# A reserve at each hand-over, and longer GpSimd steps, in a kernel whose instruction order is computed

## Chip, core and metric

The kernel runs on one NeuronCore of a Trainium2 chip. The engines named below are TensorE (PE in the profile; its weight loads are a row of their own, PEld), VectorE (DVE), ScalarE (ACT), GpSimd (POOL), and SyncE (SP), which issues most of the transfers. The metric is the device time of one execution in microseconds (us); lower is better.

## What is computed

The reference is one encoder layer on 256 tokens of width 2048, in f32, cut here to its steps:

```python
h = rms_norm(x, g_mix);  c_q, c_kv, k_rope, dq, dk, dv = split(h @ w_in)
q  = rms_norm(c_q) @ w_uq;  kv = rms_norm(c_kv) @ w_ukv        # the latents
out_mla  = softmax attention, 8 heads, rope on part of q and on k_rope
o_diff   = (softmax(q1 k1) - lam * softmax(q2 k2)) @ dv;  out_diff = rms_norm(o_diff)   # 4 heads
x = x + concat(out_mla, out_diff) @ w_out
x = x + cross_attention(rms_norm(x), rms_norm(mem)) @ w_xo     # 4 heads, 256 memory tokens
hf = rms_norm(x);  x = x + (silu(hf @ w_gate) * (hf @ w_up)) @ w_down        # hidden width 5632
return rms_norm(x)
```

## The kernel before

**Three matmuls for one product.** Every f32 operand is split in two: a high part, which is the operand rounded to the narrower type fp32r, and a low part, the remainder. A product is high x high + low x high + high x low, each a matmul with 128 rows of weights and up to 512 columns. For a weight tile the load lands in `wraw` (three buffers), ScalarE writes the high part `wh` (a CAST), VectorE subtracts to get the low part `wl` (a TENSOR_TENSOR). `wh` and `wl` have four buffers each. So each piece of weights goes DMA, ScalarE, VectorE, TensorE. The activations are split likewise: `cqT_h` and `cqT_l`, `forms_h` and `forms_l`, and so on.

**Plain and wide pieces.** A piece of kind P is used as it is. In a piece of kind W, four 512-column blocks of weights are combined into sums, `tsum` on VectorE, so that seven block products stand for eight; four of those products gather in their own PSUM tiles `q1`, `q5`, `q7`, `q6`, which VectorE later adds into the result (`left`, or `res` in the gate and up products). The sums have a longer way: DMA, VectorE (`tsum`), ScalarE (`wh<-tsum`), VectorE (`wl<-tsum`), TensorE. The last two sums of a piece use a pair of buffers of their own, `wh2` and `wl2`, shown by the profile as `wh` and `wl`. The activations that belong to W pieces have sums too (`sums`, `forms`).

**Stages.** From the start to some 40 us the input projection onto the latents; to 65 us the first differential query (`x0T` times `w_in`), beside which the latents are normalised; then MLA heads, differential heads, the output projection (from about 245 us), cross-attention (330 to 460 us), and from 460 us the feed-forward part in six chunks of hidden columns, one narrow and five wide: gate, up, then the down projection after chunks 1, 3 and 5.

**Steps named later.** `rms_rows` scales a latent by `rstd` (`cq<-acc,rstd`, `ckv<-acckv,rstd`), sums its squares on ScalarE (`ss`), adds epsilon on VectorE (`rq<-ss`, `rkv<-ss`), raises to the power -1/2 on GpSimd (`rq<-rq,mhalf`, `rkv<-rkv,mhalf`), and multiplies on VectorE (`cq<-cq,rq`). `transposed` has TensorE turn a tile into a PSUM tile `pt`, out of which VectorE multiplies by a gain (`gT<-pt,gains`) and the split follows. `kr` is the key part with rope; it needs sine and cosine, for which GpSimd computes angles in a long chain (`turns`, `prod`, `ang`) and ScalarE evaluates `sinr` and `cosr`. PSUM tiles for such use come from one ring of four (`pps`), another ring of four (`pacc`) holds the accumulators. In the differential heads `pod` is a head's output, `ssd` its mean square, `rd` the GpSimd power of it, `on` the normalised output, `pdt` its transpose. In a wide chunk, `res` (after silu and product) is turned by TensorE, copied back by ScalarE and split into `hT_h` and `hT_l`.

**What sets the order.** `Plan` records all operations with their needs, and then lays each engine's queue out by list scheduling. `cost` gives an operation the time that it keeps its engine and its lag. The first `run` takes the program's order as priority; it sets the order of matmuls (the `chain`) and which tile takes which buffer. Two more runs follow. For each, `wanted` is worked out from the end backwards: an operation is wanted when the earliest of its users is wanted, less its own lag and a fixed time where the user waits for it. Among the operations that can start within `CHOICE` = 0.3 us of the earliest, the one with the smallest `wanted` goes first. The matmuls keep the order of the run before; TensorE's transposes in the feed-forward part are `free` and find their own place. `HANDOVER` = 0.06 us is also what the simulated queues add when a result passes to another engine. The order that comes out is fixed in the program: on the chip every engine takes its instructions strictly in that order.

Of the kernel before, what the change touches and what calls it, by code (L numbers as in the profile page):

```python
# [178 lines left out]
class Plan:  # L179


    HANDOVER, CHOICE = 0.06, 0.3
    BEGUN = {"tensor": 0.6, "vector": 0.8, "scalar": 0.7, "sync": 0.7, "gpsimd": 0.3}

    def __init__(self, tc):
# [59 lines left out]
    def cost(self, engine, method, out, ins, kw):  # L245
        if method == "dma_start":
            size = max(x.cols() for x in out + ins) * 512
            return {"gpsimd": 0.55, "sync": 0.45, "scalar": 0.45}[engine], 2.0 + size / 375e3, size / 381e3
        n = max([x.cols() for x in out[:1]] + ([x.cols() for x in ins[:1]] if "reduce" in method else []))
        in_psum = bool(ins) and ins[0].tile.whole  # L250
        if engine == "tensor":
            t = 0.108 if method == "transpose" else 0.0134 + n / 2400
            return t, t + 0.14, 0.0
        if engine == "gpsimd":
            if method in ("memset", "affine_select", "tensor_copy"):
                t = 0.1 + n * 1.2e-3
            else:
                t = 0.59 if n == 1 else 0.7 if n == 2 else 1.0
            return t, t + 0.03, 0.0
        if engine == "vector":  # L260
            if n <= 16 and "reduce" not in method:
                t = 0.08
            elif method == "scalar_tensor_tensor":
                t = 0.127 + n * 1.05e-3
            elif method == "tensor_scalar":
                t = 0.129 + n * 1.035e-3 if in_psum else n / 960
            elif method == "tensor_tensor_reduce":
                t = 0.145 + n / 960
            elif method == "tensor_copy":
                t = n / 960  # L270
            else:
                t = 0.068 + n / 960
            return t, t + 0.082, 0.0
        t = 0.044 + 0.855e-3 * n if in_psum else 0.092 + 0.842e-3 * n
        if isinstance(kw.get("scale"), Ref) or isinstance(kw.get("bias"), Ref):
            t += 0.09 if n < 512 else 0.15
        if kw.get("accum_out") is not None:
            t += 0.093
        return t, t + (0.15 if kw.get("accum_out") is not None else 0.08), 0.0

    @contextmanager
    def issue_after(self, op):
        first = len(self.ops)
        yield
        for o in self.ops[first:]:
            if o.engine == op.engine:
                o.after(op, False)

    def run(self, chain, wanted, emit):
        asked = wanted is None  # L290
        for o in self.order:
# [101 lines left out]
    def emit(self, rounds=2):  # L393
        self.order = self.ops
        self.link()
        starts, ended, order = self.run(None, None, False)
        opens = {}
        for o in order:
            for h in o.tiles:
                if h.old is None:  # L400
                    continue
                if h not in opens:
                    opens[h] = done = Op("none", 0.0, 0.0, None)
                    done.number = o.number
                    for x in h.old.ops:
                        done.after(x, True)
                o.after(opens[h], True)
        self.order, seen = [], set()
        for o in order:
            for h in o.tiles:  # L410
                if h in opens and h not in seen:
                    seen.add(h)
                    self.order.append(opens[h])
            self.order.append(o)
        self.link()
        self.log = [ended]
        for n in range(rounds):
            chain = sorted((o for o in self.order if o.engine == "tensor" and not o.free), key=lambda o: starts[o])
            wanted = {}
            for o in reversed(self.order):  # L420
                wanted[o] = starts[o] if o.engine == "tensor" and not o.free else ended
                for x, waits in o.then:
                    wanted[o] = min(wanted[o], wanted[x] - (o.lag + self.HANDOVER if waits else 0.0))
            starts, ended, self.order = self.run(chain, wanted, n == rounds - 1)
            self.log.append(ended)
            self.final = starts
        for p in reversed(self.pools):
            if not p.closed:
                p.shut()
# [1038 lines left out]
```

## Time and profile before

| | |
|---|---|
| time, median of 3 runs | 1146.52 us (1145.23 to 1147.33) |
| the profiled execution | 1146.09 us, span 1144.3 us |
| TensorE matmul busy | 1128.8 us, 99% of the span |
| VectorE busy | 1016.5 us, 89% |
| ScalarE busy | 695.1 us, 61% |
| GpSimd busy | 57.7 us, 5% |
| granted TensorE clock | 0.998 of full speed |

All columns of times are in us from the start of the span. Matmuls are pipelined: a row of one matmul is some 0.39 us long, while matmuls follow each other every 0.23 us, so a busy share of 99% still holds waits. They are read from the starts of neighbouring rows. An idle time in square brackets is that of the engine just before the row, and the name behind the arrow ended it. All operations go through one helper, so all rows carry line L225, and a row is known by its tiles.

### The profile page before, as it was taken

The page shows a single profiled execution, that of the slowest core. Times are in us where ns is not written, and L with a number is a line of the kernel's source. Part 1 is how long each engine was busy: PE and PEld are TensorE (multiplying, and loading weights), DVE is VectorE, ACT ScalarE, POOL GpSimd, SP SyncE. Part 2 cuts the span into 40 slices and gives each one's busy share as a digit, 9 for nine tenths or more (in the row PEclk, how much of TensorE's full clock was granted, in tenths as well). Part 3 has the DMA queues.
Part 4 walks back from the last instruction along what each step waited for, and adds up shares of the span by engine and source line. Part 5 has one row for each costly group of instructions (what it writes and reads, how often), then busy time and mean ns, then how long its engine had stood idle before and what let it go on. Part 6 is the DMA issues. An engine that isn't in the chain of part 4 may idle for free.

```text
span 1144.3 us, 14653 instructions
## 1 busy us (share of the span) xinstructions
PE 1128.8 (99%) x5360; PEld 938.8 (82%) x5360; DVE 1016.5 (89%) x1378; ACT 695.1 (61%) x999; POOL 57.7 (5%) x75
## 2 busy tenths in 40 slices
PE   9999999999999999999999999999999999999997
PEld 7889888888888888887878888888788888888776
DVE  6688778678987776999999999999999999999995
ACT  6656455467676555756575565666655665756762
POOL 5820000010000000000000000000000000000000
PEclk9999999999999999999999999999999999999999
DMA  9643444546654444445555566456455554556453
GB/s 355 251 151 125 147 147 151 203 164 242 252 213 173 151 170 166 176 184 201 210 180 219 193 215 218 169 203 220 179 192 215 206 201 181 215 212 236 165 192 121
DMA packets 35496, 222.16 MB, mean 194 GB/s; under 512 B 4320, under 2 KB 5600, under 8 KB 11104
## 3 DMA queue, kind: packets, MB, share of 16 engines
q1 hardware_dynamic: 33696, 216.60, 52.9%
q0 software_dynamic: 864, 3.15, 0.8%
q10 hardware_dynamic: 864, 1.47, 0.4%
q8 instruction: 42, 0.69, 0.2%
q14 instruction: 30, 0.25, 0.1%
HBM read 219.11 MB, written 2.10 MB: 193 GB/s over the span
## 4 chain that ended last, share of the span: by engine, by line
PE 80%; DVE 10%; POOL 3%; issue 2%; DMA 2%; ACT 2%; SPq 0%; POOLq 0%; DVEq 0%; ACTq 0%
PE acc L225 62%; PE q L225 13%; DVE wl L225 4%; PE pt L225 2%; PE psc L225 1%; DVE tsum L225 1%; POOL prod L225 1%; PE qT L225 1%; POOL ang L225 1%; DVE res L225 1%; POOL turns L225 1%; DVE forms_l L225 1%; PE po L225 1%; DMA wraw<-in_w_dn 1%; DVE nm L225 1%
## 5 line engine op out<-in xcount | busy, mean ns | idle before, releaser
L225 ACT CAST wh<-wraw 128x1024 fp32r<-128x1024 f32 (+2 forms) x401 | 387.3, 977 | 224.8 <-PE acc L225 178.5
L225 DVE TENSOR_TENSOR wl<-wraw,wh 128x1024 fp32r<-128x1024 f32 (+2 forms) x401 | 447.7, 1130 | 83.1 <-ACT wh L225 82.0
L225 ACT CAST wh<-tsum 128x1024 fp32r<-128x1024 f32 (+1 forms) x118 | 119.6, 1017 | 127.2 <-DVE tsum L225 77.0
L225 DVE TENSOR_TENSOR wl<-tsum,wh 128x1024 fp32r<-128x1024 f32 (+1 forms) x118 | 138.1, 1174 | 7.7 <-PE acc L225 4.3
L225 PE MATMUL acc<-wh,x2n_h 128*128 128x512 f32 x320 | 124.6, 389 | 0.0
L225 PE MATMUL acc<-wh,x2n_l 128*128 128x512 f32 x320 | 124.6, 389 | 0.0
L225 PE MATMUL q<-wh,forms_h 128*128 128x512 f32 x231 | 91.2, 395 | 0.0
L225 PE MATMUL q<-wh,forms_l 128*128 128x512 f32 x231 | 90.0, 390 | 0.0
L225 PE MATMUL acc<-wh,x0T_h 128*128 128x512 f32 x224 | 88.2, 395 | 0.1
L225 PE MATMUL acc<-wl,x0T_h 128*128 128x512 f32 x224 | 88.1, 394 | 0.0
L225 PE MATMUL acc<-wh,x0T_l 128*128 128x512 f32 x224 | 87.8, 393 | 0.0
L225 PE MATMUL acc<-wl,x2n_h 128*128 128x512 f32 x320 | 86.1, 390 | 0.0
L225 PE MATMUL q<-wl,forms_h 128*128 128x512 f32 x231 | 81.0, 392 | 1.2 <-DVE wl L225 1.2
L225 DVE TENSOR_TENSOR tsum<-tsum,wraw 128x512 f32<-128x512 f32 x118 | 80.8, 684 | 0.8
L225 PE MATMUL acc<-wh,hT_l 128*128 128x512 f32 x188 | 73.8, 393 | 1.2 <-DVE hT_l L225 1.1
L225 PE MATMUL acc<-wh,forms_l 128*128 128x512 f32 x192 | 74.9, 390 | 0.0
L225 PE MATMUL acc<-wh,forms_h 128*128 128x512 f32 x192 | 74.9, 390 | 0.0
L225 DVE TENSOR_TENSOR tsum<-wraw 128x1024 f32<-128x1024 f32 (+1 forms) x64 | 72.3, 1135 | 1.9 <-DMA wraw<-in_w_out 1.0
L225 PE MATMUL acc<-wh,hT_h 128*128 128x512 f32 x188 | 73.4, 390 | 0.0
L225 PE MATMUL acc<-wl,forms_h 128*128 128x512 f32 x192 | 73.0, 390 | 0.0
L225 PEld LDWEIGHTS acc<-wh,x2n_l 128*128 128x128 f32 x320 | 60.1, 188 | 12.5
L225 PEld LDWEIGHTS acc<-wh,x2n_h 128*128 128x128 f32 x320 | 60.1, 188 | 12.4
(377 smaller groups left out, 2147.7 us busy)
## 6 DMA issues: line engine op xcount, KB each, us to landing
wraw<-in_w_gate SPq DMA_DIRECT2D x44, 1024.0 KB, 4.8
wraw<-in_w_up SPq DMA_DIRECT2D x44, 1024.0 KB, 4.8
wraw<-in_w_dn SPq DMA_DIRECT2D x41, 1024.0 KB, 4.8
wraw<-in_w_in SPq DMA_DIRECT2D x24, 1024.0 KB, 4.9
wraw<-in_w_out SPq DMA_DIRECT2D x16, 1024.0 KB, 4.9
wraw<-in_w_in_lat SPq DMA_DIRECT2D x5, 832.0 KB, 7.4
wraw<-in_w_xk SPq DMA_DIRECT2D x4, 1024.0 KB, 5.7
wraw<-in_w_xq SPq DMA_DIRECT2D x4, 1024.0 KB, 4.8
```

The source lines that it names most:

```text
L225: getattr(getattr(self.tc.nc, engine), method)(*[made(x) for x in args], **{k: made(x) for k, x in kw.items()})
```

## The change

Where `wanted` is worked out, a user that waits now costs 0.4 us (`MARGIN`) on top of the lag and not 0.06 us. The simulated queues still add 0.06 us. And GpSimd's arithmetic steps are entered as longer: 1.0 us for one or two columns (0.59 and 0.7 before), 1.2 us for more (1.0 before). No operation is added, removed or altered; the queues' order and the buffers that tiles take follow from the plan.

```diff
-    HANDOVER, CHOICE = 0.06, 0.3
+    HANDOVER, MARGIN, CHOICE = 0.06, 0.4, 0.3
...
-                t = 0.59 if n == 1 else 0.7 if n == 2 else 1.0
+                t = 1.0 if n <= 2 else 1.2
...
-                    wanted[o] = min(wanted[o], wanted[x] - (o.lag + self.HANDOVER if waits else 0.0))
+                    wanted[o] = min(wanted[o], wanted[x] - (o.lag + self.MARGIN if waits else 0.0))
```

The order moves on all engines but SyncE and the outer parts of the program. Three places are shown, and one more in words.

**TensorE where the latents are turned** (at 58 us in the profile of before, inside the first differential query). Before:

```order
L225 MATMUL pt<-ident,cq 128x128 x8
L225 MATMUL pt<-ident,ckv 128x128 x2
L225 MATMUL pt<-ident,kr 128x128 x2
L225 MATMUL acc<-wh,x0T_h 128x512
L225 MATMUL pt<-ident,ckv 128x128 x2
L225 MATMUL acc<-wl,x0T_h 128x512
L225 MATMUL acc<-wh,x0T_l 128x512
L225 MATMUL pt<-ident,kr 128x128 x2
```

After, up to the third matmul behind them:

```order
L225 MATMUL pt<-ident,cq 128x128 x8
L225 MATMUL pt<-ident,ckv 128x128 x4
L225 MATMUL acc<-wh,x0T_h 128x512
L225 MATMUL acc<-wl,x0T_h 128x512
L225 MATMUL acc<-wh,x0T_l 128x512
```

The two pairs of `ckv` now follow each other, and the four transposes of `kr` stand behind the 17th to the 21st matmul that follows.

**GpSimd at the same place**, before and after:

```order
L225 TENSOR_SCALAR ang<-prod 128x192
L225 TENSOR_TENSOR prod<-prod,ang 128x192
L225 TENSOR_TENSOR turns<-turns,prod 128x192
L225 TENSOR_SCALAR ang<-turns 128x192
L225 TENSOR_TENSOR turns<-turns,ang 128x192
L225 TENSOR_TENSOR rstd_496<-rstd_496,mhalf 128x2
L225 TENSOR_SCALAR prod<-turns 128x192
L225 TENSOR_SCALAR ang<-prod 128x192
L225 TENSOR_TENSOR prod<-prod,ang 128x192
L225 TENSOR_TENSOR rq<-rq,mhalf 128x1 x2
L225 TENSOR_TENSOR rkv<-rkv,mhalf 128x1
```

```order
L225 TENSOR_SCALAR ang<-prod 128x192
L225 TENSOR_TENSOR rstd_492<-rstd_492,mhalf 128x2
L225 TENSOR_TENSOR prod<-prod,ang 128x192
L225 TENSOR_TENSOR turns<-turns,prod 128x192
L225 TENSOR_SCALAR ang<-turns 128x192
L225 TENSOR_TENSOR turns<-turns,ang 128x192
L225 TENSOR_TENSOR rq<-rq,mhalf 128x1 x2
L225 TENSOR_SCALAR prod<-turns 128x192
L225 TENSOR_TENSOR rkv<-rkv,mhalf 128x1 x2
L225 TENSOR_SCALAR ang<-prod 128x192
L225 TENSOR_TENSOR prod<-prod,ang 128x192
```

`rstd` passes four steps of the angle chain, `rq` and `rkv` three and two; the end of the chain, which the cosines wait for, moves behind them.

**VectorE in a wide chunk, just before a down projection** (at 806 us; the same at 1057 us). Before:

```order
L225 TENSOR_TENSOR tsum<-wraw 128x1024
L225 TENSOR_TENSOR forms_l<-sums,forms_h 128x512
L225 TENSOR_TENSOR hT_l<-res_7259,hT_h 128x4x128
L225 TENSOR_TENSOR wl<-wraw,wh 128x1024
L225 TENSOR_TENSOR hT_l<-res_7287,hT_h 128x4x128
L225 TENSOR_TENSOR res_7259<-res_7259,res_6927 128x512
L225 TENSOR_TENSOR tsum<-tsum,wraw 128x512
```

After:

```order
L225 TENSOR_TENSOR tsum<-wraw 128x1024
L225 TENSOR_TENSOR hT_l<-res_7255,hT_h 128x4x128
L225 TENSOR_TENSOR res_7255<-res_7255,res_6921 128x512
L225 TENSOR_TENSOR hT_l<-res_7292,hT_h 128x4x128
L225 TENSOR_TENSOR wl<-wraw,wh 128x1024
L225 TENSOR_TENSOR tsum<-tsum,wraw 128x512
L225 TENSOR_TENSOR forms_l<-sums,forms_h 128x512
```

Both `hT_l` stand ahead of the weights' low part, and `forms_l` has gone behind.

**In words.** In the first down projection (592 us) the low part `wl2` of the last two sums, which `q6` uses, passes a `forms_l` and a `wl<-wraw` on VectorE. In the differential heads the second `rd<-ssd` on VectorE stands one step (first pair of heads) or two (second pair) earlier, ahead of an `on`, and the first transposes of `on` stand two matmuls later on TensorE. In cross-attention the fourth head's `rs` and `e` pass one `wl<-wraw` on VectorE, and its exponentials one `wh<-wraw` on ScalarE.

## The prediction

> **What bounds the kernel.** I read the first part of the page, then the windows from 461 us on, then the rows of TensorE one by one where two starts lie further apart than a matmul, and for each such gap the rows of the engine named behind the arrow.
>
> ```profile
> PE 1128.8 (99%) x5360; PEld 938.8 (82%) x5360; DVE 1016.5 (89%) x1378; ACT 695.1 (61%) x999; POOL 57.7 (5%) x75
> 284.17 22.02 PE acc L225 x97
> 461.00:600.00 139.00, 137.37 (x612) 111.84 (x611) 138.33 (x182) 90.78 (x119) 0.00 (x0) 1.00 0.53 189
> 600.00:700.00 100.00, 100.00 (x443) 82.81 (x442) 96.71 (x108) 57.08 (x63) 0.00 (x0) 1.00 0.59 208
> 800.00:840.00 40.00, 39.39 (x180) 31.69 (x179) 39.32 (x60) 27.31 (x37) 0.00 (x0) 1.00 0.46 164
> 1030.00:1105.00 75.00, 74.33 (x330) 59.71 (x329) 74.14 (x101) 52.02 (x71) 0.00 (x0) 1.00 0.57 200
> ```
>
> TensorE sets the pace: 97 matmuls in 22.02 us are 0.227 us each, and that pitch the change can't touch, since it removes no matmul. What it can take away is waits, each the distance of two starts less 0.227. The windows (columns after the length: TensorE, its loads, VectorE, ScalarE, GpSimd) show a second bound: in the feed-forward part VectorE is busy 138.33 of 139, 39.32 of 40 and 74.14 of 75 us. Before 461 us a wait that goes is time won; after it, a VectorE step can only come earlier if another comes later, and that one must not be awaited.
>
> **The latents, 59 us.**
>
> ```profile
> 59.34 0.48 PE L225 MATMUL acc<-wh,x0T_h 128*128 128x512 f32 x1
> 61.76 0.44 PE L225 MATMUL pt<-ident,ckv 128*128 128x128 f32 x2 [1.93 <-DVE gT L225]
> 47.95 0.72 POOL L225 TENSOR_TENSOR rstd<-rstd,mhalf 128x2 f32<-128x2 f32 x1
> 48.71 1.41 DVE L225 TENSOR_SCALAR cq<-acc,rstd 128x512 f32<-128x512 f32 x2 [4.44 <-POOL rstd L225]
> 57.79 0.56 POOL L225 TENSOR_TENSOR rkv<-rkv,mhalf 128x1 f32<-128x1 f32 x1
> 58.39 0.35 DVE L225 TENSOR_SCALAR ckv<-ckv,rkv 128x256 f32<-128x256 f32 x1 [1.05 <-POOL rkv L225]
> 58.66 2.44 DVE L225 TENSOR_TENSOR wl<-wraw,wh 128x1024 fp32r<-128x1024 f32 x2
> 61.02 1.27 DVE L225 TENSOR_TENSOR gT<-pt,gains 128x512 f32<-128x512 f32 x2
> 43.59 1.41 POOL L225 TENSOR_SCALAR ang<-prod 128x192 f32<-128x192 f32 x1
> ```
>
> The second pair of `ckv` takes a PSUM tile that the first `gT` has to empty; `gT` stands behind two `wl`, and these behind a wait for `rkv`. Loss: 61.76 - 59.34 - 0.23 = 2.2 us. Afterwards the pair stands next to the first, before `kr` takes the tile, and waits for no `gT`. It needs only its own `ckv`. `rstd` now follows the `ang` that ends at 45.0, so the chain starts near 45.1 and not 47.95, 2.8 us sooner, and VectorE, idle 4.44 us here, starts with it. Even if `rq` and `rkv` take GpSimd twice as long as the 0.56 us shown, the last `ckv` is done by some 57 us, two before it is needed. What becomes late is `kr`: its cosines now wait for the end of the angle chain, and that is some 2 to 4 us later; its transposes moved back by 17 matmuls or more, 3.9 us from 59.35, to 63.2. I take the full 2.2; at worst the wait returns whole.
>
> **The heads' norms, 177 and 251 us.**
>
> ```profile
> 175.82 1.62 POOL L225 TENSOR_TENSOR rd<-rd,mhalf 128x2 f32<-128x2 f32 x1 [91.27 <-DVE rd L225]
> 177.00 0.39 PE L225 MATMUL acc<-wh,x0T_h 128*128 128x512 f32 x1
> 178.11 0.30 PE L225 MATMUL pdt<-ident,on 128*128 128x128 f32 x1 [0.72 <-DVE on L225]
> 178.51 0.70 POOL L225 TENSOR_TENSOR rd<-rd,mhalf 128x2 f32<-128x2 f32 x1 [1.06 <-DVE rd L225]
> 249.24 1.23 DVE L225 TENSOR_TENSOR wl<-wraw,wh 128x1024 fp32r<-128x1024 f32 x1
> 249.30 1.71 POOL L225 TENSOR_TENSOR rd<-rd,mhalf 128x2 f32<-128x2 f32 x1 [1.13 <-DVE rd L225]
> 250.93 0.39 PE L225 MATMUL acc<-wl,mixT_h 128*128 128x512 f32 x1
> 251.68 0.30 PE L225 MATMUL pdt<-ident,on 128*128 128x128 f32 x1 [0.36 <-DVE on L225]
> ```
>
> Losses: 178.11 - 177.00 - 0.23 = 0.88 and 251.68 - 250.93 - 0.23 = 0.52 us. At 177 the first transpose stands two matmuls later, so 0.45 of the wait is filled with work and 0.43 stays, for the 1.62 us of `rd` do not shrink. The second `rd` starts 0.4 us sooner and now runs beside an `on`: if it takes 0.70 us, nothing follows; if 1.71, the second `on` comes about 0.35 late and eats most of the gain. I take 0.4, near the row of 0.70, and keep 0.1 as the lower end. The Trainium skill (GPSIMD Engine Reference, Specifications) says that GpSimd shares its SBUF interfaces with VectorE and meets contention from VectorE instructions with two SBUF inputs. That fits 1.62 and 1.71 us beside a `wl`; by that rule an `on`, whose first input lies in PSUM, leaves `rd` at 0.70 and the sum as taken. At 251 the second `rd` stands ahead of both `on`, 0.7 us sooner, and is done before the `wl` behind them ends whichever of the two durations holds; the whole 0.5 goes.
>
> **Cross-attention, 390 us.**
>
> ```profile
> 389.47 1.23 DVE L225 TENSOR_TENSOR wl<-wraw,wh 128x1024 fp32r<-128x1024 f32 x1
> 390.80 0.62 DVE L225 TENSOR_SCALAR e<-e,rs 128x256 f32<-128x256 f32 x2
> 390.68 0.40 PE L225 MATMUL acc<-wh,mT_l 128*128 128x512 f32 x1
> 391.30 0.30 PE L225 MATMUL ppt<-ident,e 128*128 128x128 f32 x1 [0.23 <-DVE e L225]
> ```
>
> 391.30 - 390.68 - 0.23 = 0.4 us, lost because `e` stands behind one `wl` of 1.14 us. With `e` ahead it goes; that `wl` belongs to weights used only several us later. Gain 0.4. So far 2.2 + 0.4 + 0.5 + 0.4 = 3.5 us.
>
> **The first down projection, 592 us.** Here VectorE is full, so a step's end moves by what is put ahead of it or taken from there.
>
> ```profile
> 590.69 0.41 DVE L225 TENSOR_TENSOR forms_l<-res,forms_h 128x256 fp32r<-128x256 f32 x1
> 591.02 1.22 DVE L225 TENSOR_TENSOR wl<-wraw,wh 128x1024 fp32r<-128x1024 f32 x1
> 592.16 1.22 DVE L225 TENSOR_TENSOR wl<-tsum,wh 128x1024 fp32r<-128x1024 f32 x1
> 592.10 0.40 PE L225 MATMUL acc<-wh,forms_l 128*128 128x512 f32 x1
> 593.43 0.50 PE L225 MATMUL q<-wl,forms_h 128*128 128x512 f32 x1 [0.94 <-DVE wl L225]
> ```
>
> TensorE loses 1.1 us here for the `wl` of 592.16, which sheds `forms_l` (0.33) and `wl` (1.14) and ends 1.47 sooner. `forms_l` goes behind it, ends 1.1 later, near 592.2, and TensorE reads it a little late, at 592.24; the awaited matmul then starts near 592.5 and not 593.43. Gain 1.0. Below: 0.3, if VectorE finds casts unfinished that it now asks for sooner; above: 1.5, the whole move.
>
> **The two later down projections, 808 and 1060 us.**
>
> ```profile
> 806.92 0.68 DVE L225 TENSOR_TENSOR forms_l<-sums,forms_h 128x512 fp32r<-128x512 f32 x1
> 809.25 0.68 DVE L225 TENSOR_TENSOR hT_l<-res,hT_h 128x512 fp32r<-128x512 f32 x1
> 807.92 0.62 ACT L225 CAST hT_h<-res 128x512 fp32r<-128x512 f32 x1
> 809.05 0.40 PE L225 MATMUL acc<-wh,hT_h 128*128 128x512 f32 x1
> 809.99 0.50 PE L225 MATMUL acc<-wh,hT_l 128*128 128x512 f32 x1 [0.55 <-DVE hT_l L225]
> 1101.53 1.23 DVE L225 TENSOR_TENSOR wl<-tsum,wh 128x1024 fp32r<-128x1024 f32 x1
> ```
>
> The gap at 809.05 is 0.7 us. The second `hT_l` sheds `forms_l` and `wl` (0.60 + 1.14) and takes `res` ahead (0.60), but its input `hT_h` ends at 808.54 and so it starts there, 0.7 us sooner: the gap closes. What was put behind is used soon, however: with 40 - 39.32 = 0.7 us of idle time in the window, VectorE can give TensorE little more than that. I take 0.6, between none and 0.9. Near 1060 the same edit meets the same rows, and at 1101.53 stands a `wl` that TensorE awaits and that has the same work ahead in both orders; only the window's 75 - 74.14 = 0.9 us can carry a gain past it. I take 0.5, from none to 0.9.
>
> **Sum.** 3.5 + 1.0 + 0.6 + 0.5 = 5.6 us, less 0.3 for new small waits where a step was put behind another (as `forms_l` at 592 us): 5.3. Between 600 and 700 us VectorE idles 3.3 us, so the 4.2 us won up to there don't run into it at once. The profiled execution took 1146.09 us (span 1144.3), 0.4 under the median of 1146.52; 1146.09 - 5.3 = 1140.8 us.
>
> **Rivals.** First, VectorE takes back the second part: what is pulled ahead there is paid at the next awaited step, and only 3.5 us are left, 1142.6 us. For it: 138.33 of 139 us busy. Against: the steps put behind at 592 and 806 us are used only after the awaited ones. Chance 0.20.
>
> Second, all the waits named go, and the gaps of 0.22 to 0.4 us beside them too: 8.2 us, 1137.9 us. Against it stands the same full VectorE. Chance 0.08.
>
> Third, the reserve does not do its work where it matters most: the chain through GpSimd is slower than even the new steps (1.62 and 1.71 us were measured where 1.0 is entered), `ckv` or `kr` arrives late and the 2.2 us of 59 us return in another place. 1146.09 - 3.1 = 1143.0 us; together with the first rival 1144.8. Against it: the 4.44 us of idle time in front. Chance 0.12.
>
> Fourth, slower: steps with two hand-overs ahead of them are pulled forward, and VectorE, strictly in order, then waits for casts that ScalarE has not done.
>
> ```profile
> L225 DVE TENSOR_TENSOR wl<-tsum,wh 128x1024 fp32r<-128x1024 f32 (+1 forms) x118 | 138.1, 1174 | 7.7 <-PE acc L225 4.3 <-ACT wh L225 2.4
> ```
>
> VectorE now loses 2.4 us before these 118 steps to ScalarE's `wh`. If each lost 0.07 us more, that is 8.3 us on a full engine: 1146.09 - 3.5 + 8.3 = 1150.9 us. It decides from 0.03 us each on, where 3.5 us are used up, and is measurably slower from 0.05. For it: on VectorE the last two sums' `wl` stands one to two steps sooner in several pieces. Against: their `tsum` stands sooner as well, and ScalarE is busy 90.78 of 139 us. Chance 0.10.
>
> **Chances and range.** The forecast has 0.50. A change under 0.2% (2.3 us) can't be told from none here. Slower by more is the fourth rival, 0.10. Within 0.2% fall the third with the first, and smaller forms of the fourth: 0.14. Faster is the rest, 0.76. The range runs from the second rival to a little past the third with the first: 1138.0 to 1145.0 us, which leaves about 2 in 10 outside.
>
> **What would show it.** In the profile after: no distance above 0.5 us between starts of TensorE near 59 us, and `kr` not awaited near 63; a wait of 0.4 us at the first `pdt` of 177 us and none at 251 and 391; at 592 and 809 us waits under 0.3 us. VectorE's busy time stays at 1016 us, for nothing was added; if its idle time from 461 to 1105 us does not fall by about 2 us, the second part of the sum is wrong. A larger idle time in front of `wl<-tsum`, ended by ScalarE, would speak for the fourth rival, a gap between 60 and 66 us ended by GpSimd or VectorE for the third.

## The result, and the profile after

The changed kernel takes 1139.55 us (median of 4 runs, 1139.03 to 1139.79) against 1146.22 us of the kernel before in the same series (4 runs, 1145.23 to 1147.33). The ratio is 0.9941, with a 95% interval of 0.9924 to 0.9958: 6.7 us faster by the medians, where 5.3 were forecast. In the later series 14 of the 37 runs of the kernel before took 1147.7 to 1148.6 us at a mean granted clock of 0.996 or 0.997, the other 23 took 1145.3 to 1147.0 us at 0.998 or 0.999, and the ratios of the experiments hold both. The profiled execution took 1139.03 us, span 1137.2, 7.1 us less than the profiled one of before.

First part of the profile's page: VectorE is busy 1.5 us less, with the same 1378 instructions. Below it, from the groups of VectorE, the one on which the fourth rival rested.

```profile
PE 1125.7 (99%) x5360; PEld 939.7 (83%) x5360; DVE 1015.0 (89%) x1378; ACT 698.8 (61%) x999; POOL 59.0 (5%) x75
...
L225 DVE TENSOR_TENSOR wl<-tsum,wh 128x1024 fp32r<-128x1024 f32 (+1 forms) x118 | 137.2, 1172 | 4.8 <-PE acc L225 3.9 <-ACT wh L225 0.6
```

The idle time that ScalarE's `wh` ends in front of these 118 steps fell from 2.4 to 0.6 us.

The waits of TensorE's matmuls (us in total, times, longest):

```profile
PE q L225 <- ACT res L225: 1.4, 2, 0.7
PE wps L225 <- DVE warm L225: 1.2, 1, 1.2
PE pt L225 <- DVE h L225: 0.5, 1, 0.5
PE po L225 <- ACT e L225: 0.5, 1, 0.5
PE po L225 <- ACT val_h L225: 0.2, 1, 0.2
```

None of the waits that the prediction names is in this list. The first and the fourth line are new: two waits for ScalarE's `res` and one for its `e`.

To see where the time came from, each matmul is paired with the same one (the same occurrence of the same tiles) of the trace of before, and the distance of the two starts is followed through the program. A step in it is time won or lost at that place; the times are those of before, but for 718 and 969 us, which are the changed kernel's own (723 and 975 us in the times of before).

| place, us | forecast | won in the traces |
|---|---|---|
| to 58 | 0 | 0.1 |
| 59, `ckv` | 2.2 | 2.1 |
| 110 to 172, MLA and differential heads | not named | 0.1 (0.6 lost at 110, 0.7 won at 121 and 172) |
| 177, `pdt` | 0.4 | 0.5 |
| 251, `pdt` | 0.5 | 0.5 |
| 390, `ppt` | 0.4 | 0.55 |
| **to 461** | **3.5** | **3.9** |
| 516 to 530 | not named | 0.2 |
| 577 to 593, first down projection | 1.0 | 1.0 |
| 718 and 969, ahead of the other two | not named | 0.8 and 0.7 lost |
| 807 to 835 | 0.6 | 1.5 |
| 1059 to 1103 | 0.5 | 2.1 |
| new small waits | -0.3 | in the lines above |
| **all** | **5.3** | **7.1** |

**59 us.** TensorE, GpSimd and VectorE of the changed kernel:

```profile
58.92 0.60 PE L225 MATMUL pt<-ident,ckv 128*128 128x128 f32 x4
59.28 0.48 PE L225 MATMUL acc<-wh,x0T_h 128*128 128x512 f32 x1
...
63.25 0.27 PE L225 MATMUL pt<-ident,kr 128*128 128x128 f32 x1
```

```profile
44.91 0.72 POOL L225 TENSOR_TENSOR rstd<-rstd,mhalf 128x2 f32<-128x2 f32 x1
...
52.77 1.89 POOL L225 TENSOR_TENSOR rkv<-rkv,mhalf 128x1 f32<-128x1 f32 x2
```

```profile
55.54 1.22 DVE L225 TENSOR_TENSOR wl<-wraw,wh 128x1024 fp32r<-128x1024 f32 x1 [1.43 <-ACT wh L225]
...
57.60 0.43 DVE L225 TENSOR_SCALAR ckv<-ckv,rkv 128x256 f32<-128x256 f32 x1
```

The four transposes stand together, 59.28 - 58.92 = 0.36 us lie between their start and the next matmul, and `kr` is not awaited. `rstd` starts at 44.91 us (forecast: near 45.1). The last `ckv` is done at 58.03 us and not by 57: of the two us of reserve that I had counted, 0.9 were there. GpSimd isn't what made it late. The two `rkv` take 1.38 and 0.55 us, together less than the twice 0.56 each that I had allowed, and are done by 54.66. On VectorE the `ckv` steps stand behind a `wl`, and this `wl` waited 1.43 us for ScalarE's cast, which the working left out.

**177 and 251 us.** GpSimd's powers and TensorE's first `pdt`:

```profile
173.42 1.63 POOL L225 TENSOR_TENSOR rd<-rd,mhalf 128x2 f32<-128x2 f32 x1 [91.17 <-DVE rd L225]
175.72 0.69 POOL L225 TENSOR_TENSOR rd<-rd,mhalf 128x2 f32<-128x2 f32 x1 [0.67 <-DVE rd L225]
...
245.83 0.69 POOL L225 TENSOR_TENSOR rd<-rd,mhalf 128x2 f32<-128x2 f32 x1 [0.44 <-DVE rd L225]
```

```profile
175.17 0.40 PE L225 MATMUL acc<-wh,x0T_l 128*128 128x512 f32 x1
175.71 0.30 PE L225 MATMUL pdt<-ident,on 128*128 128x128 f32 x1
```

0.31 us are left of the wait (175.71 - 175.17 - 0.23), forecast 0.43. The second `rd` now runs beside an `on` and takes 0.69 us, and the one of 251 us, which took 1.71 beside a `wl`, takes 0.69 as well. The Trainium skill (GPSIMD Engine Reference, Specifications) has the contention come from VectorE instructions with two SBUF inputs or in a 2-port mode. A `wl` has two SBUF inputs, while the first input of an `on` lies in PSUM; the trace agrees.

**The first down projection.** TensorE, then VectorE:

```profile
588.18 0.50 PE L225 MATMUL acc<-wh,forms_l 128*128 128x512 f32 x1
588.52 0.40 PE L225 MATMUL q<-wl,forms_h 128*128 128x512 f32 x1
```

```profile
586.58 1.22 DVE L225 TENSOR_TENSOR wl<-tsum,wh 128x1024 fp32r<-128x1024 f32 x1
587.71 0.41 DVE L225 TENSOR_TENSOR forms_l<-res,forms_h 128x256 fp32r<-128x256 f32 x1
```

The `q` that waited 1.1 us for its `wl` starts 0.34 us behind its forerunner, and `forms_l`, put behind that `wl`, is read a little late in its turn: 0.18 us too late at 584.37 and 0.13 at 588.18 (the pitch of 0.23 taken off). Both are as the prediction had them. Smaller waits from 577 us on, which were not in the sum, gave 0.3 us more.

**The second down projection.** TensorE, then VectorE, at the `hT_l` that was awaited 0.7 us at 809.99 before:

```profile
804.45 0.39 PE L225 MATMUL acc<-wh,hT_h 128*128 128x512 f32 x1
804.68 0.39 PE L225 MATMUL acc<-wh,hT_l 128*128 128x512 f32 x1
```

```profile
802.78 0.68 DVE L225 TENSOR_TENSOR hT_l<-res,hT_h 128x512 fp32r<-128x512 f32 x1
```

The last `hT_l` is done at 803.46 us, and TensorE reads it at its own pitch, 0.23 us behind the matmul before. Each of the two later down projections wins 1.2 us at its `hT_l` (the wait of 0.7 us, one of 0.2 us ahead of it, and 0.1 us behind each). The rest of the 1.5 and 2.1 us are smaller waits up to 835 and 1103 us.

**The feed-forward part as a whole**, before and after, from the windows (length; TensorE, its loads, VectorE, ScalarE, GpSimd), each from the same matmul to the same matmul:

```profile
461.00:1105.00 644.00, 641.09 (x2852) 525.99 (x2851) 632.33 (x764) 405.08 (x498) 1.10 (x2) 1.00 0.56 199
```

```profile
457.10:1098.00 640.90, 638.96 (x2854) 526.82 (x2853) 630.33 (x764) 407.99 (x499) 1.10 (x2) 1.00 0.57 200
```

The stretch is 3.1 us shorter. VectorE's idle time fell from 11.67 to 10.57 us, 1.1 us, and its busy time by 2.0 us with the same 764 instructions. Rows of VectorE that follow each other overlap by 0.08 us (the `wl` of 586.58 lasts to 587.80, the next row starts at 587.71), and behind an idle time they don't. Before, 108 of the rows stood behind an idle time, however short, now 93 do. 15 times 0.08 are 1.2 of the 2.0 us. The rows are also 0.5 us shorter in their sum, and the remaining 0.3 us are a slightly larger overlap; what makes these two is open.

**718 us**, the new wait. TensorE, then ScalarE, then ScalarE of the kernel before at the same copy:

```profile
717.52 0.60 PE L225 MATMUL pt<-ident,res 128*128 128x128 f32 x4
718.83 0.50 PE L225 MATMUL q<-wh,forms_h 128*128 128x512 f32 x1 [0.71 <-ACT res L225]
```

```profile
715.34 1.06 ACT L225 CAST wh<-wraw 128x1024 fp32r<-128x1024 f32 x1
716.29 1.06 ACT L225 CAST wh<-tsum 128x1024 fp32r<-128x1024 f32 x1
717.24 1.05 ACT L225 CAST wh<-wraw 128x1024 fp32r<-128x1024 f32 x1
718.18 0.59 ACT L225 COPY res<-pt 128x512 f32<-128x512 f32 x1
```

```profile
721.62 0.59 ACT L225 COPY res<-pt 128x512 f32<-128x512 f32 x1 [0.15 <-PE pt L225]
722.10 2.52 ACT L225 CAST wh<-wraw 128x1024 fp32r<-128x1024 f32 x3
```

`q` takes the PSUM tile that the last transposed `res` has to leave. That copy now starts behind three casts of weights, where before the casts came after it, and the transposes stand one place ahead of the `q`. 718.83 - 717.52 = 1.31 us lie between the two starts. Four transposes that nothing holds up fill 0.36 of them (as at 58.92 above), so some 0.95 are lost, and as much again at 969 us. The kernel before lost 0.2 at each of the two, so the net loss is that of the table.

### The profile page after: what moved, and what is told of

It is laid out like the page before. It is cut to its first block, busy times and chain, and to the rows that moved or that the text cites. A ratio compares the mean times of both kernels' runs of the same rounds, so it can differ in the third digit from the quotient of the medians.

```text
span 1137.2 us, 14659 instructions
## 1 busy us (share of the span) xinstructions
PE 1125.7 (99%) x5360; PEld 939.7 (83%) x5360; DVE 1015.0 (89%) x1378; ACT 698.8 (61%) x999; POOL 59.0 (5%) x75
## 4 chain that ended last, share of the span: by engine, by line
PE 95%; DVE 2%; ACT 1%; issue 1%; POOL 0%; POOLq 0%; ACTq 0%
PE acc L225 72%; PE q L225 14%; PE pt L225 2%; PE psc L225 2%; PE acckv L225 1%; PE qT L225 1%; DVE wl L225 1%; PE po L225 1%; PE kT L225 1%; PE ppt L225 1%; ACT wh L225 0%; PE wps L225 0%; DVE x2T_f L225 0%; PE pod L225 0%; ACT e L225 0%
## 5 line engine op out<-in xcount | busy, mean ns | idle before, releaser
L225 PEld LDWEIGHTS acc<-wl,x2n_h 128*128 128x128 f32 x320 | 60.1, 188 | 12.5
```

The lines of the kernel that those rows point to most:

```text
L225: getattr(getattr(self.tc.nc, engine), method)(*[made(x) for x in args], **{k: made(x) for k, x in kw.items()})
```

## Experiments

Every kernel was timed beside the kernel before. The first four take the change apart, by its two edits and by its two parts.

### The reserve without GpSimd's new steps

```diff
-                t = 1.0 if n <= 2 else 1.2
+                t = 0.59 if n == 1 else 0.7 if n == 2 else 1.0
```

> MARGIN 0.4 is kept, GpSimd's steps are entered with the old 0.59, 0.7 and 1.0 us. In this order the two pairs of ckv stand apart again and rstd stands behind the angle chain, as before the change; the steps at 251 us stand as before, those at 390 us and in the feed-forward part as after the change. Theory (each wait is won or lost at its own place): the 2.2 us at 59 us, the 0.5 at 251 us and the 0.2 before 10 us are not won, the rest is: of the 7.1 us between the two profiled executions 4.0 to 4.9 stay, 1141.2 to 1142.1 us. Rival (the reserve does it all, GpSimd's steps do not matter): 1139 to 1139.6 us, and no gap above 0.5 us near 59 us. Second rival (VectorE is full, and the feed-forward part only wins because the steps before it come earlier): at most 1 us is won, 1145 us or more.

Measured: 1141.61 us (1139.99 to 1141.68), ratio 0.995, interval 0.9937 to 0.9963. The median is the one expected, one part of its working is not:

```profile
59.74 0.48 PE L225 MATMUL acc<-wh,x0T_h 128*128 128x512 f32 x1
61.16 0.44 PE L225 MATMUL pt<-ident,ckv 128*128 128x128 f32 x2 [0.95 <-DVE gT L225]
```

The wait at 59 us is there, with TensorE in the old order, but it is 1.2 us and not 2.2: the reserve alone brings the steps ahead of it 1.0 us forward. The rest of the wait, and all that TensorE's order does there, comes from GpSimd's entries. Between 4 and 40 us TensorE lost 0.4 us more than in the kernel before; a further profile of the changed kernel (below) differs by 0.5 us there from its first.

### GpSimd's new steps without the reserve

```diff
-    HANDOVER, MARGIN, CHOICE = 0.06, 0.4, 0.3
+    HANDOVER, MARGIN, CHOICE = 0.06, 0.06, 0.3
```

> GpSimd's steps are entered with 1.0 and 1.2 us, the reserve is the old 0.06 us. Here rstd, rq, rkv and the pairs of ckv stand as after the change, and so do the first transposes of on at 177 us; the second rd stands behind both on, as before. Theory: the 2.2 us at 59 us are won and 0.2 to 0.5 at 177 us, nothing at 251 and 390 us and nothing from 461 us on: 2.2 to 3.0 us, 1143.1 to 1143.9 us. Rival (the reserve does it all): 1146 us, as before. Second rival (the change of the first part shifts the second, and what the feed-forward part wins comes from there): 1140 to 1142 us.

Measured: 1144.24 us (1143.83 to 1144.52), ratio 0.9976, interval 0.9967 to 0.9985. That is 0.3 us above the stretch given. In its trace the 2.2 us are gone, 0.45 of 0.88 us are left at 177 us, and the waits at 251, 390, 592, 807 and 1059 us are those of before within 0.1 us; the start lost 0.5 us more than before. Of the two entries it is the 1.2 us for wide steps that puts the pairs of `ckv` together: the order computed with it alone has them so, the one computed with the 1.0 us for one and two columns alone has not. Neither of the two alone was run.

### The reserve ahead of the feed-forward part alone, and in it alone

```diff
-                    wanted[o] = min(wanted[o], wanted[x] - (o.lag + self.MARGIN if waits else 0.0))
+                    margin = self.MARGIN if o.number < self.ff else self.HANDOVER
+                    wanted[o] = min(wanted[o], wanted[x] - (o.lag + margin if waits else 0.0))
...
+        plan.ff = len(plan.ops)
```

The last line stands where the narrow chunk of the feed-forward part begins.

> The reserve of 0.4 us counts for the steps up to the narrow chunk alone, 0.06 us behind it; GpSimd's steps are the new ones. Theory: the starts of TensorE run ahead by 3.9 us up to 461 us, as after the change, and by the same 3.9 us at the end, since the feed-forward part keeps its waits of 0.6, 1.1, 0.7 and 0.7 us: 1142.2 us, between 1141.6 and 1142.8. Rival (the gain of the first part runs into a full VectorE): 1143.5 us or more, with new waits on VectorE behind 461 us. Second rival (the feed-forward part gains from an earlier start alone): 1140.5 us or less.

The other kernel has `MARGIN` and `HANDOVER` exchanged in the first line, and GpSimd's old entries.

> The reserve of 0.4 us counts from the narrow chunk on, 0.06 us ahead of it; GpSimd's steps are the old ones. Theory: the first part is as before the change; in the feed-forward part the waits at 516, 592, 809, 1060 and 1102 us are taken away and two new ones of 0.9 us stand at 718 and 969 us: 3.2 us are won, 1142.9 us, between 1142.3 and 1143.5. Rival (a full VectorE takes back what is pulled ahead, and the second part wins nothing by itself): 1145.5 us or more.

Measured: 1142.39 us (1142.11 to 1142.7), ratio 0.9961, interval 0.9949 to 0.9974; and 1143.52 us (1142.4 to 1145.18), ratio 0.9974, interval 0.9964 to 0.9983. The product of the two ratios is 0.9935, that of the whole change 0.9941. The first lies in the stretch expected, the second at the upper edge of its own. So the parts add up within the intervals: what is won in front arrives at the end, and the feed-forward part wins its 3 us by itself. In the first trace the old wait for `wl` in the first down projection is there (at 589.75 us, 0.93 us idle); in the second the new one for the copy is (at 723.31 us, 0.71 us idle).

### The new waits at 718 and 969 us: products first, then copies too

Which queue makes the last copy late? Behind the line that computes `wanted`, the first kernel has

```diff
+                if o.engine == "vector" and any(x.free for x, _ in o.then):
+                    wanted[o] -= 1.0
```

> Before the down projections of 718 and 969 us the last product res<-res,res now stands behind two or three steps for weights on VectorE, its transposes stand late on TensorE, and the q behind them waits 0.9 us for ScalarE's copy. Here a product that feeds a transpose of the feed-forward part is wanted 1.0 us earlier; on VectorE it stands two steps further ahead there, its transposes two matmuls earlier on TensorE, the copies on ScalarE as after the change. Theory (VectorE's order is the cause): two matmuls, 0.45 us, come between transposes and q at each of the two places, and the wait falls to 0.4 us: 0.9 us won against the changed kernel, 1138.7 us, between 1138.2 and 1139.3. Rival (ScalarE's order is the cause, its copy stands behind a cast of weights): no gain, 1139.5 us. Second rival (VectorE is full and the weights that are put behind are awaited next): 1140 us or more.

and the second

```diff
+                if any(x.free for x in o.needs) and o.engine == "scalar" or o.engine == "vector" and any(x.free for x, _ in o.then):
+                    wanted[o] -= 0.5
```

> Product and copy are both wanted 0.5 us earlier, so the copy's place on ScalarE moves too and its needs ahead of it twice; the transposes stand five matmuls earlier on TensorE, where they stood before the change less one. Theory: both waits of 0.9 us go and nothing else is paid: 1137.8 us, between 1137.3 and 1138.4. Rival (VectorE is full, what is put behind is awaited next): 1139 us or more, with new waits on VectorE near 720 and 970 us.

Measured: 1139.39 us (1139.02 to 1139.51), ratio 0.9931, interval 0.9919 to 0.9943; and 1139.05 us (1138.69 to 1139.39), ratio 0.9929, interval 0.9916 to 0.9943. The first is the rival's result: my theory was wrong. The second missed too: 1137.3 to 1138.4 us were expected, and its runs overlap those of the first. TensorE and ScalarE of the first, then of the second:

```profile
717.52 0.60 PE L225 MATMUL pt<-ident,res 128*128 128x128 f32 x4
...
719.29 0.50 PE L225 MATMUL q<-wh,forms_h 128*128 128x512 f32 x1 [0.70 <-ACT res L225]
```

```profile
717.70 1.05 ACT L225 CAST wh<-wraw 128x1024 fp32r<-128x1024 f32 x1
718.64 0.59 ACT L225 COPY res<-pt 128x512 f32<-128x512 f32 x1
```

```profile
716.67 0.60 PE L225 MATMUL pt<-ident,res 128*128 128x128 f32 x4
...
718.45 0.49 PE L225 MATMUL q<-wh,forms_h 128*128 128x512 f32 x1 [0.25 <-ACT res L225]
```

```profile
717.82 0.58 ACT L225 COPY res<-pt 128x512 f32<-128x512 f32 x1
```

With the products alone moved, the transposes come two matmuls earlier and the `q` waits 0.87 us (719.29 less the start before it, 718.19, less 0.23), hardly less than in the changed kernel, because the copy still starts when the cast ahead of it ends (717.70 + 1.05 = 718.75, the copy's row starting 0.1 inside it). With the copies moved as well the casts end sooner against the matmuls and the wait is 0.41 us (718.45 - 717.81 - 0.23). So the wait is made by ScalarE's order; VectorE's alone doesn't remove it. The rival's new waits near 720 and 970 us did not come; of the 0.9 us that the second kernel wins at the two places, 0.5 are lost again near 1095 us.

### Copies first

```diff
+                if o.engine == "scalar" and any(x.free for x in o.needs):
+                    wanted[o] -= 0.3
```

> The copy out of a transpose of the feed-forward part is wanted 0.3 us earlier, and through it the transposes and the products ahead of it. Ahead of the down projections of 718 and 969 us the last copy now follows two casts of weights and one of a sum without a cast of hT_h between, and the transposes stand five matmuls earlier on TensorE than after the change. Theory (the last copy is late because of what stands ahead of it on ScalarE, with the product on VectorE early enough only if the transposes come early too): the copy ends some 0.5 us earlier against the matmuls than where products and copies were both moved by 0.5 us, the waits at 718 and 969 us fall under 0.2 us, and 1.4 to 1.8 us are won against the changed kernel: 1137.8 us, between 1137.4 and 1138.4. Rival (ScalarE has as many wide casts ahead of the copy as before, and so the wait stays): 1139 us or more.

Measured: 1139.18 us (1138.67 to 1139.34), ratio 0.9933, interval 0.9921 to 0.9946. Neither theory gave this: both waits are gone and the time is only 0.5 us under the 1139.66 us that the changed kernel took in the same series.

```profile
716.81 0.60 PE L225 MATMUL pt<-ident,res 128*128 128x128 f32 x4
...
718.18 0.40 PE L225 MATMUL q<-wh,forms_h 128*128 128x512 f32 x1
...
828.15 0.39 PE L225 MATMUL acc<-wh,forms_h 128*128 128x512 f32 x1
828.52 0.50 PE L225 MATMUL acc<-wh,forms_l 128*128 128x512 f32 x1
```

```profile
828.04 0.42 DVE L225 TENSOR_TENSOR forms_l<-res,forms_h 128x256 fp32r<-128x256 f32 x1
```

Against the changed kernel, TensorE wins 0.9 us at 718 us and loses 0.4 of them again from 826 to 830 us, where it waits for `forms_l` and the steps around it (0.13 us at 828.52, 0.1 at three more places). It wins 0.9 at 969 us and loses 1.0 from there to 1096 us. The window between, in this kernel's own times:

```profile
718.00:828.00 110.00, 110.00 (x494) 90.78 (x493) 109.55 (x136) 72.94 (x93) 0.00 (x0) 1.00 0.57 201
```

VectorE (the third busy time) works 109.55 of 110 us. Over the same matmuls, from 712.5 to 830.5 us, it idles 0.45 us here and 0.45 us in the changed kernel: there was next to nothing left that TensorE could have taken. That fits the first rival of the prediction, in which a full VectorE takes back what is pulled ahead; no run here frees VectorE to test it.

### Copies first, and GpSimd at the measured 1.7 us

```diff
-                t = 1.0 if n <= 2 else 1.2
+                t = 1.7 if n <= 2 else 1.2
```

> As the kernel with the copies first, and GpSimd's steps of one and two columns are entered with 1.7 us, the duration that rd had beside a wl. At 177 us both rd then stand ahead of all on on VectorE, rstd moves two steps further up on GpSimd, the transposes of kr stand 10 to 15 matmuls later. Theory (an entry that is near the measured duration takes the rest of the wait at 177 us): 0.3 us less than with the copies first alone. Rival (kr comes later still and is awaited, or the second rd runs beside a wl and takes 1.6 us): 0.5 us more or worse.

> The changed kernel itself, for a comparison on the same chip: 1139.0 to 1139.8 us, and 0.993 to 0.995 of the kernel before.

Measured: 1138.77 us (1138.5 to 1139.0), ratio 0.9931, interval 0.9919 to 0.9943, against 1139.66 us (1139.36 to 1139.78), ratio 0.9938, interval 0.9925 to 0.9952, for the changed kernel beside it. In the trace the wait at 177 us is gone and `kr`, 2.6 us later, is not awaited. Its median is 0.9 us below that of the changed kernel, and its runs lie wholly below; that it is faster than the copies alone, or than products and copies moved together, can't be said, since their runs or intervals overlap. The changed kernel's own second profile is of use too. Matched matmul by matmul it runs 0.5 us behind the first one at 40 us, and by about as much from there on: half a us at the start differs from one execution to another.

### The size of the reserve

`MARGIN` 0.2, 0.6 and 0.8, with GpSimd's new entries.

> MARGIN 0.2 and the new GpSimd steps. In this order the second rd stands at 251 us behind one on of two, at 177 us behind both, the transposes before the down projections stand as late as with 0.4. Theory (each place has its own threshold, and a place is won or not by the order alone): the 2.2 us at 59 us are won, 0.2 to 0.5 at 177 and 251 us each, 0.4 at 390 us; in the feed-forward part the waits at 592, 809 and 1060 us fall to 0.5 us or less, and the new ones of 718 and 969 us are there: 1139.5 to 1142 us. Rival (the gain grows with the reserve in proportion): half of what it gives, 1142 us or more.

> MARGIN 0.6 and the new GpSimd steps. On VectorE the sums of weights stand one or two steps further ahead than with 0.4, the steps that empty accumulators further behind. Theory (the reserve weighs kinds of steps against each other; with 0.8 the accumulators were emptied late and TensorE waited 1.2 and 3.2 us near 530 us and 3 us at 768 and 1024 us): between the two, 1140 to 1147 us, with a first wait above 1 us in the feed-forward part. Rival (flat up to the point at which a step passes another): within 0.5 us of 1139.5 us.

> MARGIN 0.8 and the new GpSimd steps: what has many hand-overs ahead of it, the sums of weights above all, is pulled far ahead of steps with few, such as those that empty PSUM tiles. Theory: the reserve is a weight between kinds of steps and has an upper end; VectorE makes weights early and results late, TensorE waits for results and for tiles, and the time is worse than with 0.4 by 2 to 12 us, 1141.5 to 1151.5 us, with waits of TensorE on VectorE behind 461 us and VectorE waiting for ScalarE's wh. Rival (more reserve covers more of what the costs leave out): 1139.5 us or less.

| reserve, us | 0.06 | 0.2 | 0.4 | 0.6 | 0.8 |
|---|---|---|---|---|---|
| time, us | 1144.24 | 1142.02 | 1139.66 | 1141.18 | 1158.04 |
| ratio | 0.9976 | 0.9955 | 0.9938 | 0.9953 | 1.0093 |
| interval | 0.9967 to 0.9985 | 0.9943 to 0.9968 | 0.9925 to 0.9952 | 0.9939 to 0.9967 | 1.0079 to 1.0107 |

The columns come from three series, each beside its own runs of the kernel before, so it is the ratios that compare.

At 0.2 the time lies at the border of the two theories and doesn't tell them apart; the places do. The waits at 251 and 1060 us are gone, three of 0.4 to 0.6 us stand in the first down projection instead of the one of 1.1, and that at 390 us is whole, against what I had read from the order (388.30 - 387.66 - 0.23 = 0.41 us).

At 0.6 the new waits of 718 and 969 us are not there, but VectorE brings another step too late, and `kr` is awaited for 0.5 us; no wait above 1 us came, as I had expected one:

```profile
585.14 0.39 PE L225 MATMUL acc<-wh,forms_h 128*128 128x512 f32 x1
586.16 0.50 PE L225 MATMUL acc<-wh,forms_l 128*128 128x512 f32 x1 [0.63 <-DVE forms_l L225]
```

At 0.8 the kernel is slower than before, more than I had allowed for. TensorE, then VectorE:

```profile
529.42 0.50 PE L225 MATMUL q<-wh,forms_h 128*128 128x512 f32 x1 [1.15 <-DVE res L225]
534.02 0.79 PE L225 MATMUL acc<-wl,forms_h 128*128 128x512 f32 x1 [3.17 <-DVE wl L225]
```

```profile
526.42 2.35 DVE L225 TENSOR_TENSOR wl<-tsum,wh 128x1024 fp32r<-128x1024 f32 x2
528.68 0.68 DVE L225 TENSOR_TENSOR res<-acc,res 128x512 f32<-128x512 f32 x1
...
531.02 2.95 DVE L225 TENSOR_TENSOR wl<-wraw,wh 128x1024 fp32r<-128x1024 f32 x3
```

Both `wl` of the sums go ahead of a `res` that TensorE needs first, then a new sum goes ahead of the plain `wl` that it needs next. VectorE has no gap there: it does the wrong work first. The same stands at 769 and 1025 us, and the three places cost 7, 5 and 5 us of the 19 that this kernel is behind the changed one in the traces. Not all of that is waiting. The window behind the second wait (length; TensorE, its loads, VectorE, ScalarE, GpSimd; then TensorE's granted clock, and two columns on DMA):

```profile
534.00:540.00 6.00, 5.98 (x14) 4.72 (x15) 4.22 (x5) 1.66 (x2) 0.00 (x0) 0.50 0.94 350
```

The granted clock is 0.50, and matmuls start 0.43 us apart (534.61, 535.04, 535.47) and not 0.23. It was 0.50 for some 3 us behind each of the other two waits as well, where the starts lie 3.2 us apart; behind the wait of 1.15 us it stayed whole. Matmuls at this pitch, counted from the starts, cost 2.9, 1.7 and 1.7 us, some 6 of the 17; the waits cost the other 11. That the long wait is what lowers the clock is read from these three places and was not varied by itself.

## Why the prediction was right, and where it was not

**The sum.** 1139.55 us lie in the range and on the right side, 1.3 us under the forecast of 1140.8. The part ahead of 461 us is right at the four places that it names; at others 0.6 us were lost and 0.7 won, and that these cancel is luck. Taken alone, with GpSimd's entries, this part gave 1142.39 us, where the prediction's own 3.5 us give 1142.6.

**59 us.** Right in size and mechanism, too sure of the reserve (0.9 us instead of two): VectorE's wait of 1.43 us for ScalarE's cast was not in the working. The experiments add what the prediction left open: TensorE's order there comes from GpSimd's entries, and the reserve is worth 1.0 of the 2.2 us by itself.

**592 us.** Right in mechanism: the wait of 1.1 us fell to 0.1, and `forms_l` took 0.3 back, as allowed for. 1.0 us net were won where the sum had 0.7, by 0.3 us of smaller waits that it didn't name.

**The term that was mis-sized** is that of the two later down projections, 0.6 + 0.5 us. I had bounded each by VectorE's idle time in its window. The places gave 1.5 and 2.1 us, 1.2 of each at its `hT_l`; two waits that I had not seen took 0.8 and 0.7 back; 2.0 us net stayed, nearly twice the 1.1. The first of the two, 0.7 net, is right by cancellation. Two steps failed. I took VectorE's busy time as fixed: of the 3.1 us by which the feed-forward part is shorter, its idle time gave 1.1 and its busy time 2.0. Of these 2.0 us 1.2 go with the 15 idle times fewer, since each costs a step the 0.08 us by which neighbours overlap, and 0.8 are not explained. My test in the last part, idle time down by 2 us, would have spoken against a term that was too small. And I followed the moved steps on VectorE alone: the copy on ScalarE that frees a PSUM tile for `q` was not in the working, though ScalarE's order moved as well.

**Rivals.** The first did not decide the sum, but it seems to be at work: with the waits of 718 and 969 us taken away, 1.4 of 1.8 us were lost again beside a VectorE with next to no gaps. Of the second, the small waits at 172, 516 and 1102 us did go, as it said; new ones kept the time above its 1137.9. The third did not come: no gap and no awaited `kr` near 63 us. The fourth came with the opposite sign at 0.4 (2.4 to 0.6 us of idle time). With 0.8 the kernel is slower, but its main loss is another mechanism than the one given: steps in the wrong order, and TensorE's halved clock behind the waits. VectorE's idle time for casts ahead of `wl<-tsum`, the sign named, did rise there to 8.4 us, but 7.7 of them come behind TensorE's waits at the three places and not ahead of them.

**Open.** What makes `po` wait 0.6 us for ScalarE's `e` at 110 us was not tried; it comes with the reserve, since it is in the kernel with the reserve alone and not in the one with GpSimd's entries alone.

## What to carry to other kernels

In a computed order a reserve per hand-over is a weight between kinds of steps: it moves those with a long way ahead of those with a short one, wins where an awaited step stood behind work with time to spare, and loses where the short way is the awaited one, so its size is found by runs (here 0.4, with 0.8 slower than none). When such an order changes, follow each awaited matmul back through every engine on its way, the copy that frees its PSUM tile included. And on an engine that is full, look at the idle times' number as well as at their sum, and be ready for a wait that is taken away to come back within the stretch that the engine fills.

## What the hardware showed

A power on GpSimd of the same two columns takes 0.69 us beside nothing or beside an `on`, and 1.63 or 1.71 us beside a `wl`. Two executions of one program differ by half a us in how TensorE starts, between 4 and 40 us. Behind three pauses of TensorE of 3.2 to 3.6 us, from start to start, its granted clock was 0.50 for some 3 to 6 us; behind one of 1.5 us it was whole. VectorE's busy time fell by 2.0 us with the same 764 instructions, of which 15 fewer idle times account for 1.2. Of these I had expected only the first.
